# Feed-forward down steps in 256-column products, with h moved 128 bytes up

## The chip, the cores and the metric

The kernel runs on one core of a Trainium2 chip. The metric is device time in microseconds (us), the median of several executions. One more execution was recorded with the hardware profiler; its page and its trace are what the text quotes. In the trace, PE is TensorE's matmuls, PEld its weight loads, DVE is VectorE, ACT ScalarE, POOL GpSimd and SP SyncE. A "matmul" is one instruction: a stationary tile of 128 rows by 128 columns, loaded beforehand by a weight load of its own, and a moving tile of up to 512 columns that streams past it.

## The reference

The program is a decoder trunk of two layers over 512 tokens of width 1024. Each layer has four sub-layers, and each is followed by a layer norm: a SwiGLU feed-forward network, a token mixer (differential attention in the first layer, a pooling mixer in the second), cross-attention into 256 memory tokens, and a second feed-forward network. The part that matters here is the feed-forward network, which occurs four times:

```
def swiglu_ffn(x, w_in, w_out):
    h = x @ w_in                      # 512 x 1024 @ 1024 x 5632
    g, u = jnp.split(h, 2, axis=-1)   # 2816 columns each
    return (jax.nn.silu(g) * u) @ w_out   # 512 x 2816 @ 2816 x 1024

x = layer_norm(a * x + 0.5 * swiglu_ffn(x, ffn_w_in[i, j], ffn_w_out[i, j]), ...)
```

All data are 32-bit floats.

## The kernel before, in words

**Products in three matmuls.** TensorE multiplies in a reduced 32-bit format (fp32r), so each operand is split into a high part, rounded to that format by ScalarE, and a low part, the rest, made by VectorE (split, L140 to L145). mm3 (L227 to L234) then issues three matmuls into the same PSUM bank: high by high (L231), high by low (L232), low by high (L233). Each matmul comes with a weight load of its own, also where the stationary tile is the same as before.

**Blocked products.** The hidden width of 2816 is taken in 11 blocks of 256. For each of them the step up (L723 and following) makes the block's h with seven block products in the manner of Strassen and Winograd in place of eight, from sums of quarters of x (the factors) and of quarters of the weights. In an up product the weights are stationary (128 columns at a time) and a factor of x moves, 256 columns (product, L752 to L764). Some of the first up products are issued in another order by by_passes (L773). The step down (L896 and following) takes two blocks of h together: the weights of 2 x 256 rows are cut into quarters b1 to b4 and combined on VectorE, seven operands are split into wh and wl, and for each operand two products (b = 0 and 1) are made. In a down product h is stationary and the split weights move, 512 columns. A product is six matmuls (two blocks k, three each), all into one PSUM bank (px or py); the pair of products of one operand, twelve matmuls, is called a down step here. VectorE adds the bank to the rows X behind each product (add, L930 to L935). The seven forms of h are made by seven (L879 to L894): ha and hb hold them as high and low parts.

**Order.** Up and down are generators. ffn (L570) drives them by a table, FFN_TURNS: two or three blocks go up in a turn while two earlier blocks go down. The steps are taken in rotation, so that up products and down steps alternate on TensorE: 48 up matmuls, 12 down matmuls, and so on, 28 down steps in each network. The last three blocks (FFN_LAST) go down without the blocked scheme in plain_down (L983 and following): xe, which by then holds h, is stationary, and the weights move, 512 columns, as wh and wl for the first half and as hb, ha for the second. TensorE executes in the order in which the program issues.

**Addresses.** Tiles lie in on-chip memory one behind the other, in the order in which their pools are opened; all tiles of this stage have sizes that are multiples of 512 bytes in each partition, so a pad decides where a tile lies modulo 512. to_w (L173) pads by apart, which is 64 here (APART, L69), ahead of the split weights wh and wl; to_x (L169) pads by 512 - apart ahead of the tiles of x. phase_pool (L178) opens the pools of a stage in the order of its keywords: for the feed-forward network (ffn_phase, L1734) b1, b3, b2, b4, then the pad of to_x, then xe, hb, sp, ha, sr and hr. So the split weights lie 64 bytes above x, modulo 512, and hb and ha lie where x lies.

Of the kernel before, what the change touches and what calls it, by code (L numbers as in the profile page):

```python
# [17 lines left out]
P = 128  # L18
D = 1024
S = 512  # L20
# [106 lines left out]
class Trunk:  # L127
# [49 lines left out]
    @contextmanager  # L177
    def phase_pool(self, gain, spare, **bufs):  # L178

        self.gain, self.spare, self.bufs, self.phase = gain, spare, bufs, {}
        with ExitStack() as ctx:
            for t in bufs:
                if t == "_x":
                    self.to_x(ctx)
                elif t == "_w":
                    self.to_w(ctx)
                else:
                    self.phase[t] = self.stage.get(t) or ctx.enter_context(self.pool(t))  # L190
            yield
# [704 lines left out]
    def down(self, pairs, w, scale):  # L896

        nc = self.nc  # L900
        r0 = pairs[0] * 2 * P
        rows = w[r0 : r0 + 4 * P].rearrange("(k c p) n -> p c k n", c=2, p=P)

        def load(i, c, half):
            t = self.tmp(f"b{i}", (P, 2, S))
            nc.sync.dma_start(t, rows[:, c - 1, :, (half - 1) * S : half * S])
            return t

        b11, b21, b12, b22 = load(1, 1, 1), load(2, 2, 1), load(3, 1, 2), load(4, 2, 2)
        yield  # L910
        hs = [self.seven_of[u] for u in pairs]

        def operand(raw):
            t = self.hl([P, 2, S])
            self.split(t[0], t[1], raw)
            return [(t[0][:, i], t[1][:, i]) for i in range(2)]

        def more(t, x):
            nc.vector.tensor_tensor(t, t, x, ALU.add)

        def product(ps, b, a, ws, start=False):

            o = slice(b * P, (b + 1) * P)
            for k in range(2):
                h, l = hs[k][a]
                self.mm3(ps, (h[:, o], l[:, o]), ws[k], start and k == 0, k == 1, not start)

        started = set()

        def add(ps, t, half):  # L930
            X = self.X[t][:, half * S : (half + 1) * S]
            by = 1.0 if (t, half) in started else scale
            started.add((t, half))
            op = ALU.subtract if half else ALU.add
            nc.vector.scalar_tensor_tensor(X, X, by, ps, ALU.mult, op)  # L935

        B = range(2)
        ws = operand(b11)
        more(b11, b12)
        xs = []  # L940
        for b in B:
            xs.append(self.aux("px", "px"))
            product(xs[b], b, 0, ws, True)
            add(xs[b], b, 0)
        yield
        ws = operand(b21)
        for b in B:
            ps = self.aux("py", "py")
            product(ps, b, 1, ws, True)
            add(ps, b, 0)  # L950
        yield
        ws = operand(b11)
        more(b11, b22)
        more(b12, b22)
        zs = []
        for b in B:
            zs.append(self.aux("pz", "py"))
            product(zs[b], b, 3, ws, True)
            add(zs[b], 2 + b, 1)
        yield  # L960
        ws = operand(b22)
        for b in B:
            product(zs[b], b, 6, ws)
            add(zs[b], b, 1)
        yield
        ws = operand(b11)
        more(b11, b21)
        for b in B:
            product(xs[b], b, 4, ws)
            add(xs[b], b, 1)  # L970
        yield
        ws = operand(b12)
        for b in B:
            product(xs[b], b, 5, ws)
            add(xs[b], 2 + b, 1)
        yield
        ws = operand(b11)
        for b in B:
            product(xs[b], b, 2, ws)
            add(xs[b], 2 + b, 0)  # L980
        yield
# [750 lines left out]
        return self.stage_pools(5, dict(raw=raw), order)  # L1732

    def ffn_phase(self, **more):  # L1734
        bufs = dict(b1=1, b3=1, b2=1, b4=1, _x=0, xe=6, hb=4, sp=4, ha=4, sr=1, hr=3)
        return self.phase_pool(("hr", "sr"), "sp", **bufs, **more)

    def ffn_first(self, layer, ln):
# [84 lines left out]
```

## Time and profile before

| | us |
|---|---|
| median of three runs (1895.87 to 1897.72) | 1897.52 |
| the profiled execution | 1899.25 |
| its span, first to last instruction | 1897.5 |

The granted TensorE clock in that execution is 0.999 of full speed. In quoted rows of groups, the columns are: line, engine, operation, output and inputs by the program's names, stationary shape, moving shape, count, then busy us and mean ns of one, then idle time of the engine ahead of them. In rows of the timeline they are: start us, duration us, engine, line, operation, names, shapes, count. Matmuls are pipelined: the duration of one contains the time until its last result is out, and the next starts long before. Rows of windows give the stretch, its length, and for each engine busy us and instructions, then the granted clock, the DMA engines' mean busy share and GB/s.

### The profile page before, as it was taken

What the parts mean: (1) busy time and instruction counts of PE and PEld (TensorE: products, weight loads), DVE (VectorE), ACT (ScalarE), POOL (GpSimd) and SP (SyncE); (2) the same over time, 40 slices, a digit from 0 to 9 for tenths busy, and PEclk for the clock granted to TensorE, in tenths of its full rate; (3) what the DMA queues carried; (4) which work ended last, traced back from release to release, by engine and by line L of the source; (5) the groups of instructions that cost most, each with busy time, mean ns of one, the idle gap of its engine ahead of it and who ended that gap; (6) DMA issues with size and microseconds to landing.
All of it is one profiled execution on the core that took longest, in us unless ns stands there. A gap on an engine that the chain in (4) does not pass through costs nothing.

```text
span 1897.5 us, 32589 instructions
## 1 busy us (share of the span) xinstructions
PE 1886.5 (99%) x13120; PEld 1730.9 (91%) x13120; DVE 1540.9 (81%) x2246; ACT 1000.8 (53%) x1542; POOL 308.2 (16%) x274
## 2 busy tenths in 40 slices
PE   9999999999999999999999999999999999999998
PEld 8999998888889988999998999999899889999996
DVE  7888989888876558889887988898786568998886
ACT  6555554566654435555554655555455436555552
POOL 3112120112110002221220311212120012211210
PEclk9999999999999999999999999999999999999999
DMA  9978772322235327987785687777464438867861
GB/s 254 215 178 178 171 141 85 103 69 75 91 112 178 112 70 181 195 177 168 144 188 168 118 179 181 168 166 162 157 172 146 142 69 180 173 159 178 185 129 53
DMA packets 250055, 283.20 MB, mean 149 GB/s; under 512 B 8752, under 2 KB 213040, under 8 KB 249904
## 3 DMA queue, kind: packets, MB, share of 16 engines
q0 software_dynamic: 94080, 94.38, 32.3%
q1 hardware_dynamic: 155824, 186.74, 30.2%
q8 instruction: 103, 1.69, 0.4%
q14 instruction: 48, 0.39, 0.1%
HBM read 274.79 MB, written 4.19 MB: 147 GB/s over the span
## 4 chain that ended last, share of the span: by engine, by line
PE 96%; DMA 2%; DVE 1%; ACT 0%; SPq 0%; issue 0%; POOL 0%; DVEq 0%; ACTq 0%
PE x L231 7%; PE x L232 7%; PE x L233 7%; PE ps L231 5%; PE ps L233 4%; PE ps L232 4%; PE z L231 4%; PE z L233 4%; PE z L232 4%; PE px L233 3%; PE px L231 3%; PE px L232 3%; PE x L773 3%; PE y L231 2%; PE y L232 2%; PE y L233 2%
## 5 line engine op out<-in xcount | busy, mean ns | idle before, releaser
L741 POOL DMA_DIRECT2D ra<-in_ffn_w_in_dram x132 | 170.7, 1307 | 977.6 <-DVE wl L748 960.4
L746 ACT CAST wh<-ra 128x1024 fp32r<-128x1024 f32 x176 | 184.9, 1053 | 197.8 <-PE x L232 63.8
L748 DVE TENSOR_TENSOR wl<-ra,wh 128x1024 fp32r<-128x1024 f32 x176 | 214.2, 1220 | 64.7 <-ACT wh L746 64.0
L231 PE MATMUL x<-xe,wh 128*128 128x256 f32 x704 | 195.0, 277 | 0.0
L232 PE MATMUL x<-xe,wh 128*128 128x256 f32 x704 | 194.8, 277 | 0.0
L233 PE MATMUL x<-xe,wl 128*128 128x256 f32 x704 | 194.8, 277 | 0.0
L746 ACT CAST wh<-rc 128x1024 fp32r<-128x1024 f32 x132 | 138.9, 1053 | 100.3 <-PE x L232 41.6
L143 ACT CAST wh<-b 128x1024 fp32r<-128x1024 f32 x112 | 117.8, 1052 | 134.8 <-PE x L232 62.2
L748 DVE TENSOR_TENSOR wl<-rc,wh 128x1024 fp32r<-128x1024 f32 x132 | 159.5, 1218 | 24.7 <-ACT wh L746 24.7
L144 DVE TENSOR_TENSOR wl<-b,wh 128x1024 fp32r<-128x1024 f32 x112 | 136.7, 1220 | 40.9 <-ACT wh L143 40.9
L231 PE MATMUL x<-xh,wh 128*128 128x256 f32 x536 | 148.7, 277 | 0.0
L232 PE MATMUL x<-xl,wh 128*128 128x256 f32 x536 | 148.4, 277 | 0.0
L233 PE MATMUL x<-xh,wl 128*128 128x256 f32 x536 | 148.4, 277 | 0.0
L231 PEld LDWEIGHTS x<-xe,wh 128*128 128x128 f32 x704 | 132.4, 188 | 1.3
L232 PEld LDWEIGHTS x<-xe,wh 128*128 128x128 f32 x704 | 132.3, 188 | 1.3
L233 PEld LDWEIGHTS x<-xe,wl 128*128 128x128 f32 x704 | 132.2, 188 | 0.0
L144 DVE TENSOR_TENSOR wl<-raw,wh 128x1024 fp32r<-128x1024 f32 x64 | 78.5, 1233 | 45.8 <-ACT wh L143 45.2
L231 PEld LDWEIGHTS x<-xh,wh 128*128 128x128 f32 x536 | 100.8, 188 | 0.7
L232 PEld LDWEIGHTS x<-xl,wh 128*128 128x128 f32 x536 | 100.8, 188 | 0.7
L233 PEld LDWEIGHTS x<-xh,wl 128*128 128x128 f32 x536 | 100.7, 188 | 0.0
L143 ACT CAST wh<-raw 128x1024 fp32r<-128x1024 f32 x64 | 66.4, 1049 | 62.5 <-PE xq L232 18.2
L231 PE MATMUL z<-xe,wh 128*128 128x256 f32 x352 | 97.5, 277 | 0.0
(445 smaller groups left out, 6239.9 us busy)
## 6 DMA issues: line engine op xcount, KB each, us to landing
ra<-in_ffn_w_in_dram POOLq DMA_DIRECT2D x132, 512.0 KB, 7.0
rc<-in_ffn_w_in_dram SPq DMA_DIRECT2D x88, 512.0 KB, 5.8
b<-in_ffn_w_out_dram SPq DMA_DIRECT2D x76, 512.0 KB, 5.0
ra<-in_ffn_w_in_dram SPq DMA_DIRECT2D x44, 512.0 KB, 4.7
rc<-in_ffn_w_in_dram POOLq DMA_DIRECT2D x44, 512.0 KB, 7.3
raw<-in_xa_wkv_dram SPq DMA_DIRECT2D x16, 1024.0 KB, 5.4
raw<-in_da_w_qkv_dram SPq DMA_DIRECT2D x24, 512.0 KB, 3.7
raw<-in_xa_wq_dram SPq DMA_DIRECT2D x8, 1024.0 KB, 5.2
```

The lines of the kernel that those rows point to most:

```text
L143: self.nc.scalar.copy(hi, src),
L144: self.nc.vector.tensor_sub(lo, src, hi.bitcast(F32)),
L231: self.first_mm = mm(out, w[0], x[0], start=start, stop=False, skip_group_check=again)
L232: mm(out, w[0], x[1], start=False, stop=False, skip_group_check=again)
L233: self.last_mm = mm(out, w[1], x[0], start=False, stop=stop, skip_group_check=again)
L741: nc.gpsimd.dma_start(t, source(*block), accum_op=ALU.add)
L746: hi = nc.scalar.copy(v[0], raw)
L748: lo = nc.vector.tensor_sub(v[1], raw, v[0].bitcast(F32))
L773: self.last_mm = nc.tensor.matmul(ps[:, j], v[i][:, k, j * P : (j + 1) * P], x[l][:, k], start=n == i == l == 0, stop=n == 7 and i == 1, s ...
```

## The change

A down product is made in two halves of the columns, 0 to 255 and 256 to 511, each a 256-column matmul for every stationary tile; both halves go into the same bank, the start flag stands on the first matmul alone and the stop flag on the last. A new keyword "_h" in phase_pool pads by twice apart, 128 bytes, and ffn_phase puts it behind xe and ahead of hb. So hb, sp, ha, sr and hr lie 128 bytes higher, and hb and ha 64 bytes above the split weights, modulo 512. xe stays.

```
                 elif t == "_w":
                     self.to_w(ctx)
+                elif t == "_h":
+                    self.pad(ctx, 2 * self.apart)
                 else:
...
         def product(ps, b, a, ws, start=False):

             o = slice(b * P, (b + 1) * P)
-            for k in range(2):
-                h, l = hs[k][a]
-                self.mm3(ps, (h[:, o], l[:, o]), ws[k], start and k == 0, k == 1, not start)
+            for c, e in ((0, 2 * P), (2 * P, S)):
+                for k in range(2):
+                    h, l = hs[k][a]
+                    self.mm3(
+                        ps[:, c:e], (h[:, o], l[:, o]), [w[:, c:e] for w in ws[k]],
+                        start and c == k == 0, k == 1 and e == S, True,
+                    )
...
     def ffn_phase(self, **more):
-        bufs = dict(b1=1, b3=1, b2=1, b4=1, _x=0, xe=6, hb=4, sp=4, ha=4, sr=1, hr=3)
+        bufs = dict(b1=1, b3=1, b2=1, b4=1, _x=0, xe=6, _h=0, hb=4, sp=4, ha=4, sr=1, hr=3)
```

## The prediction

> **What bounds the kernel now.** I read the page's busy table and chain first, then the feed-forward stretches by windows, then the groups by form, then the matmul starts one by one, since the change touches only how matmuls follow each other.
>
> ```profile
> span 1897.5 us, 32589 instructions
> PE 1886.5 (99%) x13120; PEld 1730.9 (91%) x13120; DVE 1540.9 (81%) x2246; ACT 1000.8 (53%) x1542; POOL 308.2 (16%) x274
> PE 96%; DMA 2%; DVE 1%; ACT 0%; SPq 0%; issue 0%; POOL 0%; DVEq 0%; ACTq 0%
> ```
> ```profile
> core 0: us, PE busy (x) PEld busy (x) DVE busy (x) ACT busy (x) POOL busy (x), PEclk, DMA share, GB/s
> 801.00:1018.00 217.00, 217.00 (x1601) 204.59 (x1600) 189.26 (x232) 115.92 (x139) 38.57 (x30) 1.00 0.74 161
> ```
>
> TensorE is busy in 99% of the span and is 96% of the chain that ended last. The second row is one of the four feed-forward networks, in the stretch where up and down steps alternate: TensorE has no gap in 217 us, VectorE works 189 us of it (87%), the DMA engines 74%. So a nanosecond won or lost in the spacing of matmuls is a nanosecond of the kernel, as long as it stays under the 13% that VectorE has to spare.
>
> The durations of single matmuls overlap and tell little; the distance from start to start is what counts. These are rows of TensorE's timeline where an up product, a down step and an up product follow each other:
>
> ```profile
> 1839.89 0.28 PE L233 MATMUL x<-xe,wl 128*128 128x256 f32 x1
> 1840.00 0.39 PE L231 MATMUL pz<-wh,hb 128*128 128x512 f32 x1
> ...
> 1842.75 0.28 PE L231 MATMUL x<-xh,wh 128*128 128x256 f32 x1
> ...
> 1843.34 0.28 PE L233 MATMUL x<-xh,wl 128*128 128x256 f32 x1
> ...
> 1848.10 0.28 PE L233 MATMUL x<-xh,wl 128*128 128x256 f32 x1
> 1848.21 0.39 PE L231 MATMUL px<-wh,hb 128*128 128x512 f32 x1
> ```
>
> Three things stand in it. The twelve down matmuls of a step (one 512-column operand each, two halves of h times two row blocks times three) take 2.75 us, 229.2 ns each. The up matmuls from the sixth on take (1848.21 - 1843.34)/43 = 113.3 ns, so two of 256 columns cost 226.6 ns where one of 512 costs 229.2. And the first five up matmuls behind the down step take 0.59 us, 118 ns each: about 0.025 us is lost whenever TensorE comes back from a down step. At the step's other edge nothing is lost (0.11 us from 1839.89 to 1840.00).
>
> **The change, part by part.** *Number of products.* Every matmul of the down steps becomes two:
>
> ```profile
> L231 PE MATMUL px<-wh,hb 128*128 128x512 f32 x192 | 75.1, 391 | 0.1
> L231 PE MATMUL pz<-wh,hb 128*128 128x512 f32 x128 | 49.7, 388 | 0.0
> L231 PE MATMUL px<-wh,ha 128*128 128x512 f32 x64 | 24.9, 389 | 0.0
> L231 PE MATMUL py<-wh,ha 128*128 128x512 f32 x64 | 24.9, 388 | 0.0
> ```
>
> That is 448 per line and 1344 over the three lines of mm3, or 112 steps of twelve (28 in each network). Afterwards there are 112 steps of 24, with 1344 more weight loads.
>
> *Their pace.* In an up product the stationary weights lie 64 bytes above the moving x, modulo 512 (the pads to_w and to_x). In a down step h is stationary and the weights move, and h lies where x lies, so the difference is -64. With the 128-byte pad h comes 64 above the weights: a down matmul then has the up matmul's width, operand type and address difference. I give it the up pace. A step: 24 x 113.3 ns = 2.72 us instead of 2.75, 0.028 us less before rounding (229.0 against 226.7 per pair), times 112 = -3.1 us.
>
> *The way back.* Nothing in a down step then differs in shape from an up product, so the five slow matmuls behind it should go. By the starts in the trace they follow 91 of the 112 steps (the last of them at 1842.75 above, the first at 79.63 below; the other steps are followed by a down step or by the plain part): 91 x 0.025 = -2.3 us. A check of both terms over sixteen whole rounds of an up product and a down step:
>
> ```profile
> 109.73 0.39 PE L231 MATMUL px<-wh,hb 128*128 128x512 f32 x1
> ...
> 241.14 0.39 PE L231 MATMUL px<-wh,hb 128*128 128x512 f32 x1
> ```
>
> 131.41/16 = 8.213 us for a round; 72 matmuls at 113.3 ns are 8.160. The 0.053 us is 0.028 plus 0.025.
>
> *The swaps.* At each edge of a step the roles turn over: for one matmul the next stationary tile lies 128 bytes above the moving one (into a step), then 0 (out of it), instead of 64. The trace has the 0 case (1839.89 to 1840.00, no loss) but no 128. Bounds: nothing, or the 0.025 us of today's way back, at 224 edges (0 to +5.6 us). I take 4 ns an edge, +0.9 us, near the lower bound, because both neighbours in address (64 and 0) cost nothing while the pace is fast.
>
> *The plain part.* Three blocks of each network are multiplied plainly, with xe stationary; there hb and ha are the moving tiles of the second half of the columns:
>
> ```profile
> L231 PE MATMUL ps<-hb,xe 128*128 128x512 f32 x60 | 23.6, 396 | 0.0
> L231 PE MATMUL ps<-ha,xe 128*128 128x512 f32 x30 | 11.7, 389 | 0.0
> ```
>
> Today xe and hb lie alike modulo 512; the pad makes the difference -128, which the trace has nowhere. There are 270 such matmuls of 512 columns. The paces of that width nearby run from 229.2 ns (above) to 233.3 (the step 76.83 to 79.63 below, 2.80/12), so up to 270 x 4 ns = 1.1 us either way. I take 0.
>
> *The rest.* The products keep their sums, their order by step, their buffers and the VectorE additions, which still wait for the last matmul into the same bank. No wait and no transfer of data is added. Instruction fetch grows:
>
> ```profile
> q8 instruction: 103, 1.69, 0.4%
> ```
>
> 2688 instructions more than 32589 are 8%, 0.14 MB and 0.03% of the DMA engines, beside queues that run at 74%: nothing. sp, ha, hb, sr and hr all move by 128 bytes; VectorE and ScalarE read them at full lines as before, with 13% of slack or more.
>
> The sum: -3.1 - 2.3 + 0.9 = -4.5 us. The profiled execution took 1899.25 us, 1.75 around its span of 1897.5; it would take 1894.75. The median of the runs shown is 1897.52, 1.73 below it, so the forecast is 1893.0 us. A measurement of this kernel can tell about 0.2% (3.8 us) from no change.
>
> *A rule against the split.* The two rows above give 113.3 ns for 256 columns and at least twice that for 512, so a matmul carries no fixed cost that a split would pay again. The Trainium skill (TensorE: Matmul & The Clock Gate, section "Wait — 56ns, not 53.3ns?") states one: some 2.5 ns per warm matmul whatever its width. By it, as an estimate, the split would add 1344 x 2.5 ns = 3.4 us. The rows don't bear it out here.
>
> **The rivals.** The weak point is that the same matmul has two paces. In the first network TensorE once had to wait, and then this came:
>
> ```profile
> 34.32 0.38 PE L773 MATMUL z<-xh,wh 128*128 128x256 f32 x1
> 34.54 0.28 PE L773 MATMUL z<-xl,wh 128*128 128x256 f32 x1
> ...
> 45.73 0.28 PE L231 MATMUL x<-xe,wh 128*128 128x256 f32 x1
> ...
> 76.83 0.40 PE L231 MATMUL px<-wh,ha 128*128 128x512 f32 x1
> ...
> 79.63 0.28 PE L231 MATMUL y<-xh,wh 128*128 128x256 f32 x1
> ...
> 80.22 0.28 PE L233 MATMUL y<-xh,wl 128*128 128x256 f32 x1
> 80.33 0.28 PE L231 MATMUL y<-xh,wh 128*128 128x256 f32 x1
> ```
> ```profile
> 769.67 0.28 PE L231 MATMUL x<-xe,wh 128*128 128x256 f32 x1
> ...
> 799.60 0.39 PE L231 MATMUL px<-wh,ha 128*128 128x512 f32 x1
> ```
>
> From 45.73 to 76.83 are 264 up matmuls, 117.8 ns each; the same 264 in the third network (769.67 to 799.60) take 113.4. Tiles, shapes and address differences are equal; only how TensorE came into the run differs. The slow pace holds until something breaks it, and what broke it at 76.83 was the first 512-column step: five matmuls behind it the pace is 0.11. The change takes all such steps away.
>
> *Slow in the first network.* If the new down steps don't break the slow pace, its remaining 28 rounds of 72 run 4.4 ns slow: 2016 x 4.4 = +8.9 us against the fast pace, which is +7.4 against now (28 x 0.053 = 1.5 less). The other three networks still win (0.75 x 4.5 = 3.4). Net about +4.0, 1901.5 us. For it: no row shows a swap of 256-column products ending the slow pace at equal differences. Against: a wait of TensorE, of which there are some, changes it too.
>
> *A swap throws TensorE into the slow pace.* This is the other side, slower. The mixer of the second layer has such swaps, between memory keys (pk, weights stationary, +64) and pooled products (ps, weights moving, -64):
>
> ```profile
> 1425.31 0.28 PE L231 MATMUL pk<-mem2h,wh 128*128 128x256 f32 x1
> ...
> 1425.99 0.28 PE L231 MATMUL ps<-wh,pooled 128*128 128x256 f32 x1
> ...
> 1427.36 0.28 PE L231 MATMUL pk<-mem4h,wh 128*128 128x256 f32 x1
> ...
> 1431.24 0.28 PE L231 MATMUL xq<-xh,wh 128*128 128x256 f32 x1
> ```
>
> Six pk at 113.3, twelve ps at 114.2, and then, with no wait between, 33 pk at 117.6 that stay slow. So a swap can do it. Against: there the difference jumps from +64 to -64 and back, here it is +64 on both sides. The price depends on where it falls. Only the down halves slow: 2688 x 4.4 - 5.4 = +6.4, 1904 us. Only the up halves: 5376 x 4.4 - 5.4 = +18, 1916 us. Both: +30, 1928 us. It decides from the twelfth slow matmul of a round of 72 on (0.053/0.0044).
>
> *The swaps cost what the way back costs now.* 0.025 us at both edges eats the gain: -5.4 + 5.6, 1897.7 us.
>
> *A fixed cost per matmul,* the rule above as a mechanism: the extra weight load or start costs something that the up rows hide. Halves would then take more than 229.2/2 = 114.6 ns. The slowest halves in the rows take 117.8, 6.4 ns more for a pair; half of that, 3.2 ns x 1344, is +4.3 us, less the 2.3 of the way back: 1899.5 us. Against it stand all up rows at 113.3, which load weights for every 256 columns too.
>
> **How the numbers follow.** The forecast 0.48; slow in the first network 0.17; a swap into the slow pace 0.20; swaps that eat the gain 0.10; the fixed cost 0.05. The forecast's own range is 1890.5 (no loss at the edges and 1.1 us from the plain part, and the scatter of the runs) to 1895.5. The range over the cases takes in the first network's rival and the cheapest form of the swaps: 1890.5 to 1904.5; up halves in the slow pace, some 0.15, are left out. Faster by over 0.2%: most of the forecast, 0.48, with a little of it on the border. Within 0.2%: the eaten gain, the fixed cost's border, and half of the first network's case (+4.0 lies on the line): 0.22. Slower: 0.30.
>
> **What would show it.** Right: down rows of 128x256, 24 to a step, at 113.3 ns start to start; the first five up matmuls behind a step at 113.3 too; a round of 8.16 us in all four networks. Wrong: a distance of 117 to 118 that stays, in the down rows or in the up rows behind them; a first network whose rounds take longer than the others'; 0.23 or more from a first half to the next product. The plain rows ps<-hb,xe and ps<-ha,xe show the pad's side effect. If VectorE waits for nothing and TensorE shows gaps, the cover was thinner than I took it.

## The result, and the profile after

The changed kernel takes 1909.20 us (median of six executions, 1907.84 to 1911.01), the kernel before 1897.62 us (six, 1895.87 to 1898.49): a ratio of 1.0062, 95% interval 1.0049 to 1.0075, so 11.6 us or 0.62% slower. The forecast was 1893.0, and the range ended at 1904.5. The profiled execution took 1908.16 us, span 1906.4, against 1899.25 and 1897.5 before. (Nine of 41 executions of the kernel before that were made beside later experiments took 1904.1 to 1906.3 us, the others 1895.7 to 1901.4; none of the nine was profiled, so an experiment with a single execution is read from its trace.) These are the lines of the changed kernel's page that answer to the first fence of the prediction:

```profile
span 1906.4 us, 35268 instructions
PE 1893.3 (99%) x14464; PEld 1792.7 (94%) x14464; DVE 1542.8 (81%) x2246; ACT 999.8 (52%) x1542; POOL 307.9 (16%) x274
PE 95%; DVE 2%; DMA 2%; issue 0%; ACT 0%; SPq 0%; POOL 0%; DVEq 0%; POOLq 0%; ACTq 0%
```

There are 1344 matmuls more, as the diff says. TensorE is still 99% busy and still the chain; VectorE's work is the same. So most of the loss is in the spacing of matmuls, where the gain was to be. TensorE's timeline, where an up product, a down step and an up product follow each other (up, its sixth matmul, down, up):

```profile
1842.95 0.29 PE L233 MATMUL x<-xe,wh 128*128 128x256 f32 x1
...
1843.54 0.28 PE L235 MATMUL x<-xe,wl 128*128 128x256 f32 x1
...
1848.42 0.28 PE L233 MATMUL pz<-wh,hb 128*128 128x256 f32 x1
...
1851.24 0.29 PE L233 MATMUL x<-xh,wh 128*128 128x256 f32 x1
```

The down step of 24 halves takes 2.82 us, 117.5 ns each; it was 2.75 with twelve whole products and was to be 2.72. The 43 up matmuls from the sixth on take (1848.42 - 1843.54)/43 = 113.5 ns, and the first five 0.59 us, 118 ns each, just as before. So the down halves run at the slower of the two paces, and the way back costs what it did. Sixteen rounds in the first network say the same:

```profile
109.23 0.28 PE L233 MATMUL px<-wh,hb 128*128 128x256 f32 x1
...
241.81 0.28 PE L233 MATMUL px<-wh,hb 128*128 128x256 f32 x1
```

132.58/16 = 8.286 us a round, against 8.213 before: 0.073 us more at each of 112 steps, +8.2 us.

The second, smaller loss is a wait, in the plain part of the first network:

```profile
299.02 0.40 PE L233 MATMUL ps<-wh,xe 128*128 128x512 f32 x1
300.90 0.36 PE L233 MATMUL px<-wh,hb 128*128 128x256 f32 x1 [1.48 <-DVE X L941]
```

TensorE wants the bank of px and waits 1.5 us for VectorE's addition out of it. The kernel before at the same place:

```profile
297.90 0.39 PE L231 MATMUL ps<-wh,xe 128*128 128x512 f32 x1
298.39 0.47 PE L231 MATMUL px<-wh,hb 128*128 128x512 f32 x1
```

There the start is 0.49 us behind the one ahead of it, against 1.88 us in the changed kernel: 1.4 us less.

Adding the distances from each matmul's start to the next over both traces splits the 8.9 us between the spans: down steps 308.1 before, 316.1 after (+8.0); up products -1.3; the plain part +3.6 (this wait 1.4, the rows that read ha and hb 0.9, the rest other short waits); everything else -1.3. (The medians lie 11.6 apart: the profiled execution of before is 1.6 us above its median, the one of after 1.0 below.) Nearly all of the up products' -1.3 (1.2) is the run of 264 up matmuls ahead of the first step:

```profile
46.16 0.28 PE L233 MATMUL x<-xe,wh 128*128 128x256 f32 x1
...
76.08 0.28 PE L233 MATMUL px<-wh,ha 128*128 128x256 f32 x1
```

29.92 us, 113.3 ns each; in the trace of before it was in the slow pace (117.8). The change touches nothing there.

### The profile page after: what moved, and what is told of

Its sections match the earlier page's. It is cut to its first block, busy times and chain, and to the rows that moved or that the text cites. A ratio compares the mean times of both kernels' runs of the same rounds, so it can differ in the third digit from the quotient of the medians.

```text
span 1906.4 us, 35268 instructions
## 1 busy us (share of the span) xinstructions
PE 1893.3 (99%) x14464; PEld 1792.7 (94%) x14464; DVE 1542.8 (81%) x2246; ACT 999.8 (52%) x1542; POOL 307.9 (16%) x274
## 4 chain that ended last, share of the span: by engine, by line
PE 95%; DVE 2%; DMA 2%; issue 0%; ACT 0%; SPq 0%; POOL 0%; DVEq 0%; POOLq 0%; ACTq 0%
PE x L235 7%; PE x L233 7%; PE x L234 7%; PE ps L233 5%; PE ps L234 5%; PE ps L235 5%; PE z L233 4%; PE z L234 4%; PE z L235 4%; PE px L233 3%; PE px L235 3%; PE px L234 3%; PE x L775 3%; PE y L233 2%; PE y L235 2%; PE y L234 2%
## 5 line engine op out<-in xcount | busy, mean ns | idle before, releaser
L143 ACT CAST wh<-b 128x1024 fp32r<-128x1024 f32 x112 | 117.7, 1051 | 128.3 <-PE x L234 63.0
L233 PE MATMUL px<-wh,hb 128*128 128x256 f32 x384 | 107.9, 281 | 1.7 <-DVE X L941 1.5
L234 PE MATMUL px<-wl,hb 128*128 128x256 f32 x384 | 107.7, 281 | 0.0
L235 PE MATMUL px<-wh,hb 128*128 128x256 f32 x384 | 107.7, 281 | 0.0
```

The source lines that it names most:

```text
L143: self.nc.scalar.copy(hi, src),
L233: self.first_mm = mm(out, w[0], x[0], start=start, stop=False, skip_group_check=again)
L234: mm(out, w[0], x[1], start=False, stop=False, skip_group_check=again)
L235: self.last_mm = mm(out, w[1], x[0], start=False, stop=stop, skip_group_check=again)
```

## The experiments

The question is why the same matmul takes 113.3 ns in one place and 117.7 in another. Theory A: what decides is the one matmul at an edge between up and down, at which the address difference between the next stationary and the moving tile jumps (in the changed kernel it is +64 bytes in the steps, but +128 into a down step and 0 out of it); the pace that TensorE is in behind the edge is then kept as long as matmuls follow each other alike. Theory B: 256-column products with h stationary are slow of themselves. All differences are modulo 512; "into" is how far h lies above x, "in" how far h lies above the down weights, "out" how far the up weights lie above the down weights. Below, the slow pace is some 117.7 ns for 256 columns, the fast one 113.3.

### split_only: the halves without the pad

```
-        bufs = dict(b1=1, b3=1, b2=1, b4=1, _x=0, xe=6, _h=0, hb=4, sp=4, ha=4, sr=1, hr=3)
+        bufs = dict(b1=1, b3=1, b2=1, b4=1, _x=0, xe=6, hb=4, sp=4, ha=4, sr=1, hr=3)
```

> The down products in 256-column halves, without the pad: h lies 64 bytes below the weights, as before. Theory A (what decides is the one matmul at the edge of a down step, during which the next stationary tile is fetched from an address 128 bytes above the moving tile; in the changed kernel it throws TensorE from 113.3 to 117.6 ns): here that difference is 0 at both edges, which cost nothing before, so the first down step behind a fast up product runs at 113.3. On the way back the rows of the second layer's mixer (fast at -64, then slow at +64 for 33 matmuls) say that the up product then turns slow, so up rows of 117.7 appear: about 1905 to 1916 us. Theory B (a 256-column product with h stationary is slow of itself, whatever the addresses): down rows at 117.6 in every step, up rows as in the changed kernel, about 1906 to 1909 us with the pad's effect on the plain part gone.

Measured: 1914.37 us (1912.50 to 1915.16) against 1898.29 before, 1.0085, interval 1.0071 to 1.0099. The starts of four steps in a row, down, up, down, up, down:

```profile
802.26 0.28 PE L233 MATMUL px<-wh,ha 128*128 128x256 f32 x1
...
804.98 0.28 PE L233 MATMUL y<-xh,wh 128*128 128x256 f32 x1
...
810.64 0.28 PE L233 MATMUL py<-wh,ha 128*128 128x256 f32 x1
...
813.47 0.28 PE L233 MATMUL z<-xh,wh 128*128 128x256 f32 x1
...
818.92 0.28 PE L233 MATMUL pz<-wh,hb 128*128 128x256 f32 x1
```

The down step at 802.26 takes 2.72 us (113.3 ns a half), the up product behind it 5.66 (117.9), the next down step 2.83 (117.9), the next up product 5.45 (113.5): one round fast into slow, the next slow into fast, for most of the network. Halves with h stationary can run at 113.3 ns, here at a difference of -64 within the step. The pace is carried into the step (difference 0 at that edge, -64 behind it) and turned over at the way out (0, then +64), in both directions.

### pad_only: the pad without the halves

```
+                elif t == "_h":
+                    self.pad(ctx, 2 * self.apart)
...
+        bufs = dict(b1=1, b3=1, b2=1, b4=1, _x=0, xe=6, _h=0, hb=4, sp=4, ha=4, sr=1, hr=3)
```

> The pad alone, down products 512 columns wide, h 64 bytes above the weights. Theory A and its rule of differences: the second layer's queries run 512 columns at +64 and take 233.3 ns each, so the 1344 down matmuls cost 4.3 ns more than the 229 of before, +5.8 us; and the plain part, with hb and ha moving 128 bytes above xe, costs what it cost in the changed kernel, about +1 us: 1903 to 1905 us. Theory B (addresses do nothing for these products): 229 ns and 1897.6 us.

Measured: 1914.08 us (1913.44 to 1915.96), 1.0087, interval 1.0073 to 1.0101. Down, up, down, up, down:

```profile
833.99 0.39 PE L233 MATMUL px<-wh,hb 128*128 128x512 f32 x1
...
836.78 0.28 PE L233 MATMUL x<-xe,wh 128*128 128x256 f32 x1
...
842.43 0.39 PE L233 MATMUL px<-wh,hb 128*128 128x512 f32 x1
...
845.23 0.28 PE L233 MATMUL x<-xh,wh 128*128 128x256 f32 x1
...
850.70 0.39 PE L233 MATMUL px<-wh,hb 128*128 128x512 f32 x1
```

The whole products take 2.79 and 2.80 us a step (232.5 and 233.3 ns; 229.2 before), and every second up product is slow (5.65 against 5.47). So the +64 that the pad brings into the step is no better for 512 columns than -64 but worse, and the pad alone costs more than the whole change. The expectation had the slower steps (they cost +5.1 us between the traces) and not the slow up products (+10.1), and so missed by 9 us.

### level_512: a pad of 64 bytes, whole products

```
+                elif t == "_h":
+                    self.pad(ctx, self.apart)
```

> Half the pad (64 bytes), down products 512 columns wide: h lies where the weights lie, and the next stationary tile is 64 bytes above the moving one on the way in and 0 on the way out. Theory A: the plain rows of 512 columns with xe and ha lying alike ran at 226.7 ns, so the 1344 down matmuls cost 2.4 ns less, -3.2 us; the way back is open: with no slow up rows another -2.3 us (1892), with the slow pace in all up products +18 (1913). Theory B: 229 ns, 1897.6 us.

Measured: 1917.90 us (1917.41 to 1919.51), 1.0107, interval 1.0093 to 1.0121. Up, down, up:

```profile
830.65 0.28 PE L233 MATMUL x<-xe,wh 128*128 128x256 f32 x1
...
836.30 0.39 PE L233 MATMUL px<-wh,hb 128*128 128x512 f32 x1
...
839.02 0.28 PE L233 MATMUL x<-xe,wh 128*128 128x256 f32 x1
```

At a difference of 0 the down step takes 2.72 us, 226.7 ns a product: the fastest whole products of all runs, and exactly two fast halves. But every up product is slow from end to end (5.65 us, 117.7 ns). The steps gain 2.9 us and the up products lose 21.5: here what a step does to the pace of its neighbours outweighs its own cost.

### even_64: +64 at the edges too, in one network

Only in the second network: halves; the weights of the down steps start 448 bytes into their buffers, which are made larger by 512 bytes, and h is moved by 64 bytes. Then into, in and out are all +64. Elsewhere the kernel is the one before.

```
+    def hl(self, shape, lower=False):
+        if self.roomy:
+            o, n = (ROUND - self.apart) // 4 if lower else 0, shape[1] * shape[2]
+            return tuple(
+                self.stage[t].tile([P, D + P], F32R, tag=t, name=t, bufs=self.w_bufs)[:, o : o + n]
...
-            t = self.hl([P, 2, S])
+            t = self.hl([P, 2, S], True)
```

> In the second feed-forward network alone, the down products are split in halves, and the down step's weights lie 448 bytes higher in buffers of 4608 bytes, h 64 above them: so every stationary tile, in the steps and at both edges, lies exactly 64 bytes above the tile that moves while it is fetched. The other three networks are as before. Theory A: in that network up and down rows all run at 113.3 ns with no slow matmuls at either edge, a round of 72 takes 8.16 us in place of 8.213; the total gains 28 x 0.053 = 1.5 us, too little to see in one time. Theory B: down rows at 117.6 and a round of about 8.28.

Measured: 1897.20 us in one execution, span 1895.4. Down, up, down in the second network:

```profile
831.10 0.28 PE L233 MATMUL px<-wh,hb 128*128 128x256 f32 x1
...
833.82 0.28 PE L233 MATMUL x<-xe,wh 128*128 128x256 f32 x1
...
839.26 0.28 PE L233 MATMUL px<-wh,hb 128*128 128x256 f32 x1
```

2.72 and 5.44 us, 8.16 a round: the round that the prediction had promised, with no slow matmul at either edge. Shape, operands and the difference within the step are those of the changed kernel; the edges differ. That rules theory B out and shows that the changed kernel lost its pace to where h and the down weights were put. As x and the up weights stay where they are, the jump at an edge can't be moved without moving h or the down weights, so no run tells the jump from the place itself; for the jump speaks that in split_only, and in even_all below, the same places carry both paces.

### even_all, even_512, raw_three, level_split

even_all does the same in all four networks. For room, three of them get three buffers for raw weights (ra) in place of four. even_512 has the same addresses with whole products, raw_three is the kernel before with the three buffers alone, and level_split is the pad of 64 bytes with halves (into +64, in 0, out 0).

```
-        return self.stage_pools(4, dict(ra=4, rc=3), ("wh", "wl", "ra", "rc"))
+        return self.stage_pools(4, dict(ra=self.raws, rc=3), ("wh", "wl", "ra", "rc"))
...
+        self.roomy, self.raws = (layer, 0) in EVEN, 3
...
+        self.roomy, self.raws = (layer, 1) in EVEN, 3 if layer else 4
```

> In all four networks now: the down products split into halves of 256 columns, the weights of the down steps 448 bytes into their buffers, so that the next stationary tile lies 64 bytes above the moving one (modulo 512) at every matmul of the up and down steps, edges included. Three of the networks give up one of four buffers for raw weights to make room. If the pace hangs on this difference alone, every up and down row runs at 113.3 ns and a round of 72 takes 8.16 us in all four networks: 112 x 0.053 = 5.9 us less than before at most, less some 1.5 us for the wait in the first network that the split brought through another order on VectorE: 1892 to 1894.5 where the kernel before takes 1898. If halves with h stationary are slow of themselves, 1904 or more. If a buffer for raw weights is missed, waits of TensorE for weights appear and the control tells their size.

> The same addresses as even_all, with the down products left at 512 columns. If the address difference is all that counts, a 512-column matmul takes two fast halves (226.7 ns), the five slow up matmuls behind each step go, and the gain is that of even_all without the changed order on VectorE: 1892 to 1893. If the split is needed (a change of width at an edge costs something of its own), the 512-column rows stay at 229 ns or the up rows behind them start slow: 1895 to 1898.

> The kernel before with three buffers for raw weights in place of four in the same three networks, and nothing else. No theory of the pace says anything but no change (1896 to 1899); if it is slower, that is the price of the buffer that even_all and even_512 carry too.

> A pad of 64 bytes and the split: h lies at the weights' residue, so the difference is +64 into a down step, 0 within it and 0 out of it. If the difference behind the last matmul of a step (0 in place of +64) throws the up product into the slow pace, as it seemed with 512 columns, the down rows take 113.3 ns and the up rows 117.7 as there: 1915 to 1919. If the change of width was what did it there, the up rows here are fast and the time is 1892 to 1895.

Measured, beside 1897.61 us for the kernel before:

| | us | ratio, 95% interval |
|---|---|---|
| even_all | 1914.89 (1911.38 to 1918.72) | 1.0080, 1.0057 to 1.0102 |
| even_512 | 1907.88 (1905.70 to 1909.31) | 1.0043, 1.0028 to 1.0059 |
| raw_three | 1899.17 (1898.30 to 1904.11) | 1.0003, 0.9989 to 1.0016 |
| level_split | 1912.03 (one execution) | |

The expectation for even_all missed by 20 us, that for even_512 by 10. The profiled execution of even_all is its fastest, 1911.38; what the slower ones, up to 1918.72, lose on top is not known. In its trace the first (but for waits), second and fourth networks run as promised; here is the second, and then the third, in which a run of up products leads to the first down step:

```profile
801.95 0.28 PE L234 MATMUL px<-wh,ha 128*128 128x256 f32 x1
...
804.67 0.28 PE L234 MATMUL y<-xh,wh 128*128 128x256 f32 x1
...
1070.74 0.28 PE L234 MATMUL y<-xh,wh 128*128 128x256 f32 x1
...
1127.27 0.28 PE L234 MATMUL px<-wh,ha 128*128 128x256 f32 x1
...
1130.10 0.28 PE L234 MATMUL y<-xh,wh 128*128 128x256 f32 x1
...
1135.75 0.28 PE L234 MATMUL py<-wh,ha 128*128 128x256 f32 x1
```

2.72 us for the step in the second network; in the third the 480 up matmuls from 1070.74 take 56.53 us (117.8 ns), and the pace does not end: 2.83 and 5.65, 8.48 a round, through all down and up rows that alternate. What brings TensorE into this run slow is open: level_512, even_512 and even_reset have it there too, the other traces don't. Equal differences do not make TensorE fast; they keep the pace that it has, the slow one too. even_512 shows one thing that ends it:

```profile
1071.15 0.28 PE L234 MATMUL y<-xh,wh 128*128 128x256 f32 x1
...
1127.69 0.40 PE L234 MATMUL px<-wh,ha 128*128 128x512 f32 x1
...
1130.49 0.28 PE L234 MATMUL y<-xh,wh 128*128 128x256 f32 x1
...
1135.94 0.39 PE L234 MATMUL py<-wh,ha 128*128 128x512 f32 x1
```

The same run is as slow (56.54 us), and behind the first whole step the up product is fast (5.45) and stays so. But whole products at +64 take 2.80 us a step, 233 ns, which is 0.05 more than in the kernel before, at 112 steps 5.5 us of the 9.6 between the spans.

level_split tells that the entry need not be +128: down at 803.14, up at 806.01, down at 811.47.

```profile
803.14 0.28 PE L233 MATMUL px<-wh,ha 128*128 128x256 f32 x1
...
806.01 0.29 PE L233 MATMUL y<-xh,wh 128*128 128x256 f32 x1
...
811.47 0.28 PE L233 MATMUL py<-wh,ha 128*128 128x256 f32 x1
```

2.87 us for the step, 119.6 ns a half (slower than the slow pace elsewhere), and 5.46 for the up product. Both its expectations fell: the down rows are slow and the up rows fast, the opposite of level_512 at the same addresses.

raw_three's time can't be told from that of the kernel before; its interval allows 3 us. Its trace has two waits in the first network, 0.3 us each, at 71.98 and 89.01, which the kernel before has not; even_all and even_512 have the first of them too, at 1.2 and 1.0 us. So the missing buffer is at most a small part of what the two pay. In both, the pooling mixer behind the third network also takes some 3 us longer (187.9 and 188.7 us between the networks, 185.2 before); 1.4 and 2.1 us of it are waits for VectorE's split weights and for transfers of the memory tokens, of which the kernel before has none there. Why they come was not followed.

### even_reset and even_two_reset: one whole step to begin with

even_all with the first down step of a network left whole, in all four networks, and the same in the second and the fourth alone.

```
+            self.whole -= 1
-            for c, e in ((0, 2 * P), (2 * P, S)) if self.roomy else ((0, S),):
+            for c, e in ((0, 2 * P), (2 * P, S)) if self.roomy and self.whole < 0 else ((0, S),):
```

> even_all with the first down step of each network left at 512 columns. In even_all three networks ran at 113.3 ns throughout, and the third kept the pace of 117.7 ns with which it entered its run of up products, through every up and down row to its end; in even_512 the first 512-column step behind the same slow run ended it. If the pace is inherited while every matmul has the same width and address difference, and a 512-column step breaks the slow one, all rounds behind the first step take 8.16 us in all four networks, also where the run ahead of it is slow: the third network loses its 27 x 0.32 = 8.6 us, 1906 us against 1915 for even_all. If the third network is slow for a reason of its own (its addresses, its buffers), it stays at 8.48 us a round and the time at 1912 to 1917.

> The same in the second and the fourth network alone; the other two as in the kernel before. Two networks at 8.16 us a round instead of 8.213: 2 x 27 x 0.053 = 2.9 us less, 1894.7 where the kernel before takes 1897.6, if nothing else moves. If the fourth network's larger buffers bring the waits in the mixer ahead of it that even_all and even_512 had (some 3 us), the gain is gone: 1897 to 1899.

Measured: even_reset 1909.85 us (1903.73 to 1911.96) against 1898.52, 1.0044, interval 1.0029 to 1.0060; even_two_reset 1898.52 us, 0.9997, interval 0.9983 to 1.0010. The third network of even_reset: run of up products, whole step, up, the next step:

```profile
1076.84 0.28 PE L234 MATMUL y<-xh,wh 128*128 128x256 f32 x1
...
1133.37 0.40 PE L234 MATMUL px<-wh,ha 128*128 128x512 f32 x1
...
1136.17 0.28 PE L234 MATMUL y<-xh,wh 128*128 128x256 f32 x1
...
1141.62 0.28 PE L234 MATMUL py<-wh,ha 128*128 128x256 f32 x1
```

The run is slow again (56.53 us), the whole step ends it, and from there the rows are fast (5.45 for the up product) to the end of the network, as expected. The 8.6 us did not come whole, in good part because the first network did the opposite in this trace. Its whole step was a round past, the rows were fast, and then, without any change of address difference, a matmul started late twice; the slow pace behind that held for the rest of the network:

```profile
89.30 0.28 PE L234 MATMUL z<-xh,wh 128*128 128x256 f32 x1
...
91.23 0.28 PE L236 MATMUL z<-xh,wl 128*128 128x256 f32 x1
91.39 0.36 PE L234 MATMUL z<-xh,wh 128*128 128x256 f32 x1
91.59 0.28 PE L235 MATMUL z<-xl,wh 128*128 128x256 f32 x1
...
94.30 0.28 PE L234 MATMUL pz<-wh,hb 128*128 128x256 f32 x1
...
97.12 0.28 PE L234 MATMUL z<-xe,wh 128*128 128x256 f32 x1
```

Up to 91.23 the distance is 113.5 ns (1.93/17), then 0.16 and 0.20 us, too little for the trace to name a releaser, and from 91.59 on (94.30 - 91.59)/23 = 117.8. The next step takes 2.82. Behind a halt of a tenth of a microsecond TensorE stays slow for the next 200 us. A halt need not do this: a longer one, a wait of 0.34 us at 88.52, had left the rows fast within four matmuls. And one can end the slow pace: in the first network of even_all the rows are slow behind a wait of 0.41 us at 89.08 (117.8 ns), and fast again behind a start that came 0.05 us late at 92.14, at equal differences throughout. The times of this kernel lie in two groups, four from 1903.7 to 1905.7 and five from 1909.9 to 1912.0; that this is the first network fast or slow fits their distance, but only one execution was profiled.

even_two_reset runs both its networks at 8.16. Its span is 1895.9 against 1897.5, and the timed runs can't tell it from the kernel before.

### edges: other jumps at the edges

even_all's code in the second and fourth networks, with +64 within the steps, but +96 into and +32 out of a step in the second, 0 into and +128 out of it in the fourth.

```
-                    self.pad(ctx, self.apart if self.roomy else 0)
+                    self.pad(ctx, self.lift)
...
-            o, n = (ROUND - self.apart) // 4 if lower else 0, shape[1] * shape[2]
+            o, n = (ROUND - 2 * self.apart + self.lift) // 4 if lower else 0, shape[1] * shape[2]
...
+        self.lift = 0 if layer else 96
```

> Split products in the second and the fourth network alone, with +64 in every up and down step as in the changed kernel, but other jumps at the edges: in the second network +96 into a step and +32 out of it, in the fourth 0 into it and +128 out of it (the changed kernel has +128 and 0, even_all +64 and +64). If any edge unlike +64 turns the pace over, both networks show down rows at 117.7 ns and up rows at 113.3 ns behind some five slow ones, 8.29 us a round, as the changed kernel does. If only a jump as wide as 64 bytes does, the second network runs at 113.3 ns throughout (8.16 us). If the 128 of the entry alone turns it and a 0 does nothing, the fourth network's down rows are fast, and its up rows behind the 128 slow (8.37 us).

Measured: 1907.21 us in one execution beside 1898.26. Down, up, down in the second network; up, down, up in the fourth:

```profile
831.32 0.28 PE L234 MATMUL px<-wh,hb 128*128 128x256 f32 x1
...
834.14 0.28 PE L234 MATMUL x<-xe,wh 128*128 128x256 f32 x1
...
839.62 0.28 PE L234 MATMUL px<-wh,hb 128*128 128x256 f32 x1
...
1662.53 0.28 PE L234 MATMUL x<-xe,wh 128*128 128x256 f32 x1
...
1668.18 0.29 PE L234 MATMUL px<-wh,hb 128*128 128x256 f32 x1
...
1670.93 0.28 PE L234 MATMUL x<-xe,wh 128*128 128x256 f32 x1
```

The second network is the changed kernel's pattern: slow down rows (2.82) and fast up rows behind some slow matmuls (5.48). The fourth has it the other way round: slow up rows (5.65), fast down rows (2.75, slower only at the start). So with edges that differ from +64 by 32 or by 64 bytes the pace is set anew. The third case of the expectation has the fourth network's pattern (8.37 us a round; it took 8.40), but its reason falls: +96 and +32 turn the pace over in the second network, and in the fourth an entry of 0 turned slow into fast. No case has both networks. Every arrangement of halves that was run, side by side:

| into, in, out | down halves | up behind them |
|---|---|---|
| +128, +64, 0 (changed kernel) | slow | fast after three or four |
| +96, +64, +32 (edges, second network) | slow | fast after five |
| +64, +64, +64 (even_64, even_all) | keep the pace they find | keep it |
| 0, +64, +128 (edges, fourth network) | fast after three or four, where they find it slow | slow |
| 0, -64, 0 (split_only) | keep the pace they find | the other pace |
| +64, 0, 0 (level_split) | slow (119.6 ns) | fast after three or four |

## Why the prediction was wrong, point by point

*The step that failed: the swaps.* The prediction gave an edge 4 ns, "because both neighbours in address (64 and 0) cost nothing while the pace is fast". The edge itself costs nearly that little: in the changed kernel the first half behind it is 0.11 to 0.12 us away. What it does is set the pace of all 24 halves behind it. A step takes 2.82 us in place of 2.72, some 0.10 us, where the upper bound was 0.025; 112 x 0.10 is +11 us in place of +0.9; with the -3.1 of the halves that makes the steps' +8.0 in the trace. The bound was taken from the way back, whose loss ends after five matmuls; the sum did not ask whether a loss at the other edge would end, though one of the rivals did. The row with a difference of 0 and "no loss" led into a 512-column step, and the experiments show that those follow other rules. And it was one edge of two: by the prediction's own addresses the way out of a step lay at 0 in the kernel before as well (both tiles there are weights), and its row is the one that loses 0.025 us. So 0 had not been free.

*Number and pace of the halves.* The pace behind the -3.1 us exists: 2.72 us stands in even_64, even_all and split_only. The reason given for it, the difference of +64 within the step, was wrong: split_only reaches the same 2.72 at -64, and whole products are slowest at +64 (233 ns in even_512), faster at -64 (229.2 before, apart from the first step, which came out of slow up products and took 233.3), fastest at 0 (226.7 in level_512).

*The way back.* The -2.3 us did not come: the first five up matmuls still take 0.59 us. The prediction laid these slow matmuls to the shape of the step, but the width is not what makes them: in even_512 whole products stand ahead of 48 up matmuls that take 5.45 us, and with halves and the same edges it is 5.44 (even_64). In the kernel before and in the changed one the way out lies at 0, which the pad does not touch; with +64 there, as in even_64 and even_512, they are gone. (The slow matmuls follow 99 steps in the trace of before, not 91, so the term would have been -2.5.)

*The plain part.* Taken at 0, with 1.1 us either way; the rows that read ha and hb came out at +0.9, inside the bounds.

*The rest.* "No wait and no transfer of data is added" was wrong. Splitting doubles the matmuls of a step, and the program that results has VectorE's and ScalarE's instructions in another order than before (the order of pad_only and level_512, which have whole products, is unchanged). The wait of 1.5 us for X in the first network stands in the changed kernel, as 1.3 us in split_only and level_split, as 2.1 in even_all and 1.0 in even_reset, which all have halves there; where the first network has none it is some 0.1 us or less. That the new order is its cause was not tried by itself.

*The rivals.* "A swap throws TensorE into the slow pace", in its form with only the down halves slow, is what happened; its forms had a part of 0.20 together, and this one was priced at +6.4 us. By the prediction's own terms the price lacked the 2.3 us of the way back, which it had credited: with them the steps come to +8.7, beside +8.0 in the trace. The plain part, +3.6 in the trace, was in no price of it. The range ended at 1904.5 and so left no room for either. "Slow in the first network" did not happen in this trace, but its mechanism, a slow pace that steps of halves do not end, is what even_all shows. (The 264 fast matmuls from 769.67 to 799.60 that it was held against lie in the second network, not in the third; the comparison stands.) The fixed cost per matmul is ruled out by level_512: a whole product of 226.7 ns equals two halves of 113.3.

## What to carry to other kernels

Where TensorE is the bound and its rows show two paces for one shape, price a change by what it does to the pace of the rows behind each edge, not by the edge: a loss that ends after five matmuls and one that lasts to the next edge look the same in the row at the edge. A row of one width is no evidence for the edges of another. And a step that looks slow by itself may be what brings its neighbours back to the fast pace: the whole products of the kernel before cost 2.5 ns more than two fast halves, and the rows behind them were fast again after five matmuls.

## What the runs showed of the hardware

A 256-column matmul takes 113.3 ns or 117.7 ns at equal shape, operands, address difference and granted clock (0.999 in every profile here): in one up product of even_reset the rows ran at 113.5 ahead of a halt and at 117.8 behind it. The pace can be kept over hundreds of matmuls (480 at 117.8 ahead of the third network's first step in even_all); other address differences at the edges, or a halt, can set it anew. Only addresses and history differ, and every matmul comes with a weight load (0.19 us in these traces) that runs beside the matmul ahead of it, so an interplay of the two reads is a possible cause; no run took the weight loads away, so it stays argued. The Trainium skill (TensorE: Matmul & The Clock Gate, section "Step-by-step: what each phase is for") says that loading the next tile's weights takes no read bandwidth from the running matmul. No run here measures that; the two paces, 113.3 and 117.7 ns, only show that the time of a matmul here is not settled by its shape and clock. Which jump leads to which pace has no rule yet that fits every line of the table above.
